# A hybrid DeltaNet and attention layer on one core: the first projection chunk in full fp32, the output projection by tokens, and the residual copied into the down projection's accumulators

## The chip, the cores and the metric

One core of a Trainium2 chip runs the whole layer. The metric is the time in microseconds from the first to the last moment of one execution on the device; three runs of the kernel before took 1507.93, 1508.70 and 1508.71 us (median 1508.7). The engines are TensorE (PE), VectorE (DVE), ScalarE (ACT) and GpSimd (POOL); SyncE (SP) issues most of the DMAs. Each engine works through a queue of its own in order, and engines wait for each other by semaphores.

## The reference

A decoder layer on 256 tokens (T) with 2048 channels (D), all in fp32. Two branches start from one projection of the normed input, are merged by sigmoid gates and go through an output projection; a gated MLP with a short convolution follows.

```python
h = rms_norm(x, ln1)
qkv_a, beta_a, decay_a, z_a, qkv_b, gate_a, gate_b = split_columns(h @ w_in)
y_a = gated_deltanet(qkv_a, beta_a, decay_a, z_a, ...) @ w_branch_a   # 8 heads of 128, causal conv of 4
y_b = moba_attention(q_b, k_b, v_b) @ w_branch_b                       # 8 heads of 128, partial rotary
x = x + (sigmoid(gate_a) * y_a + sigmoid(gate_b) * y_b) @ w_out
h = rms_norm(x, ln2)
u_gate, u_val = split(causal_dwconv(h @ w_up, ffn_conv, ffn_conv_bias))  # w_up is 2048 x 11264
x = x + (silu(u_gate) * u_val) @ w_down                                  # w_down is 5632 x 2048
return rms_norm(x, final_norm)
```

In the DeltaNet branch, a decay per head and token is `-exp(a_log) * softplus(a_logit + dt_bias)`, summed up along the tokens.

## The kernel before

**Matmuls.** The weights come from HBM as fp32 and each operand of a large matmul is split in two parts of type fp32r: a rounded high part and the rest. ScalarE makes the high part of a weight (`act.copy`, the CAST `wh<-wraw` of L118), VectorE the rest (`wl<-wraw,wh`, L115), and PE adds three products: high by high, high by rest, rest by high. `fetch` loads 1 MB of weights into one of four `wraw` buffers, `load_w` splits it in pieces. There are two ways to multiply:

- `chunk`: two blocks of 128 output channels. The weight is the stationary operand, the activations move, 256 tokens (or, where the PSUM pool is `wide`, high and rest side by side as 512 columns, so that two matmuls do the three products). The result has channels on the partitions.
- `by_token`: 512 output channels at a time. A tile of 128 tokens is stationary, the weights move 512 columns at a time. The result has tokens on the partitions.

**The norm.** The activations are only scaled by ln1 (`scaled`: high part on ScalarE L216, rest on VectorE L217, into `hc`). The factor of RMSNorm, R1, is applied to the results: by `join`, which copies and multiplies a chunk's PSUM result (tiles `un`, `unf`), or by a column `cols` of it per token. The sums of squares come from GpSimd (three pieces and one sum, L290 and L293) and ScalarE (one, L292); PE adds them over the partitions with two fp32 matmuls against `ones` (`R`), and a sqrt and a reciprocal follow.

**Stages in order.** (1) The input `xs` comes channel-major in eight pieces of 256 KB, alternating with eight pieces of the first two blocks of `w_gdn`; chunk q of DeltaNet group 0 is computed while they land (`ps_q0`). Then the small projection for beta and decay (`ps_bd`), R1, chunk k and chunk v; the decay chain on VectorE; a few small transposes (`pt_cols`) that turn decay, beta and R1 into columns. (2) For four groups of two heads: chunks q, k, v, and for every second group z by tokens (`ps_z`); then a generator `gdn` with the DeltaNet recurrence. (3) Four groups of MoBA attention (`ps_moba`, `ps_v`), also with generators. (4) Gates and branch projections by tokens (`ps_gate`, `ps_br`), merged and transposed (`pt_m`) to `mc`. (5) Output projection by chunks (`ps_wo`), residual added, squares, R2. (6) 44 up chunks (`ps_up`), convolution, silu, product into `acts`. (7) Down projection in eight PSUM banks `pd[i][n]`, 128 tokens by 512 channels each; the residual is transposed into them on PE by four 128x128 transposes a bank (L814). Then the last norm.

**What sets the order.** Instructions go out in program order unless a scheduler moves them by estimated times and priorities. Generators in the list `bg` (gdn, moba, rotary, merged) are advanced by `tick`, once for every 1700 ns of main matmuls (`main_mm`), so that their small instructions lie between the large matmuls. `while len(bg) > 1: tick()` after the third MoBA group runs all DeltaNet generators to their end, because the pool `gdn_st` is closed there and its space taken by the gates' tiles.

Of the kernel before, what the change touches and what calls it, by code (L numbers as in the profile page):

```python
# [11 lines left out]
F32 = mybir.dt.float32  # L12
# [7 lines left out]
P = 128  # L20
# [60 lines left out]
def layer_kernel(ctx: ExitStack, tc: tile.TileContext, xT, pos, cst, csel, ceye, vec, convw, ffw, bdv,  # L81
# [51 lines left out]
    def load_w(src, n=2048, into=None, piece=1024, raw=None):  # L133
        raw = raw or fetch(src, n)
        wh, wl = into or parts()
        for o in range(0, n, piece):
            split(wh[:, o:o + piece], wl[:, o:o + piece], raw[:, o:o + piece])
# [104 lines left out]
    wq = []  # L242
    for b in range(2):
        raw = wpool.tile([P, 2048], F32, name="wraw", tag="wraw", bufs=4)
        wq.append((raw, *parts()))
    for i in range(4):
        s = slice(4 * i, 4 * i + 4)
        for b in range(2):
            h = slice(4 * i + 2 * b, 4 * i + 2 * b + 2)
            sp.dma_start(xs[:, h, :], xT[:, h, :])  # L250
            sp.dma_start(wq[b][0][:, 512 * i:512 * i + 512], w_gdn[b][:, 512 * i:512 * i + 512])
    ps_q0 = mmt("ps_gdn")
    for i in range(4):
        scaled(xs[:, 4 * i:4 * i + 4, :], ln1v, 4 * i, hh, hl)
        for b in range(2):
            raw, wh, wl = (t[:, 512 * i:512 * i + 512] for t in wq[b])
            split(wh, wl, raw)
            for k in range(4):
                a = 4 * i + k
                main_mm(ps_q0[:, b], r3(wh, P)[:, k], hh[:, a], a == b == 0, False)  # L260
                main_mm(ps_q0[:, b], r3(wh, P)[:, k], hl[:, a], False, False)
                main_mm(ps_q0[:, b], r3(wl, P)[:, k], hh[:, a], False, a == KD - 1)
# [4 lines left out]
    raws = [fetch(w) for w in (w_gdn[2], w_gdn[3])]  # L267
# [15 lines left out]


    sq = []
    for i in range(4):
        sq.append(g.tile([P, 4, T], F32, name=f"sq1_{i}"))
        xv = xs[:, 4 * i:4 * i + 4, :]
        if i < 3:
            pool.tensor_tensor(sq[i], xv, xv, op=ALU.mult)  # L290
        else:
            act.activation(sq[i], xv, AF.Square)  # L292
    pool.tensor_tensor(sq[0], sq[0], sq[1], op=ALU.add)  # L293
# [639 lines left out]
```

## Time and profile before

| what | value |
|---|---|
| median of 3 runs | 1508.7 us (1507.93 to 1508.71) |
| the profiled execution, its time and its span | 1508.24 us, 1506.5 us |
| mean granted clock of TensorE | 0.996 |
| PE busy | 1482.6 us (98%) |
| DVE, ACT, POOL busy | 991.3 us (66%), 743.4 us (49%), 172.4 us (11%) |
| DMA traffic | 276.84 MB, mean 184 GB/s |

The span is the time between the first and the last instruction of the profiled execution; its own time is 1.7 us longer. Busy times are sums over the span, so a share of 66% can hold a stretch of 20 us in which the engine is never idle. Matmuls overlap each other in the records: the time that one costs is the distance between two starts, not its duration.

### The profile page before, as it was taken

The numbers are of one execution on the slowest core, as the hardware profiler recorded it, in microseconds if no ns is written. First come the engines' busy times: TensorE is split into PE (matmuls) and PEld (weight loads), VectorE is DVE, ScalarE is ACT, GpSimd is POOL, SyncE is SP. The second block draws the span as 40 slices with busy tenths as digits, with TensorE's granted clock in tenths as the row PEclk, the third lists the DMA queues.
The fourth block names the chain that finished last, engine by engine and source line by source line (L and its number), as shares of the span: only waits on it lengthen the run. The fifth ranks groups of instructions, "written<-read, shape, count | busy, mean of one in ns | idle before, by whom it ended". The sixth has DMA issues, their size and how long they took to land.

```text
span 1506.5 us, 21027 instructions
## 1 busy us (share of the span) xinstructions
PE 1482.6 (98%) x8507; PEld 1305.9 (87%) x8507; DVE 991.3 (66%) x1413; ACT 743.4 (49%) x997; POOL 172.4 (11%) x130
## 2 busy tenths in 40 slices
PE   7999999999999999999999999999999999999997
PEld 7899899998988888888888888888888888888886
DVE  8888668796655444666667677676776765555554
ACT  5565454435474444434455555554555554444444
POOL 3011001141203000000101212112111120000000
PEclk9999999999999999999999999999999999999999
DMA  8355444444445555546555555555555544555552
GB/s 312 141 198 190 163 154 157 149 169 147 154 154 174 193 194 194 193 177 249 186 208 196 184 188 188 196 196 182 188 189 196 196 177 162 195 195 194 195 196 84
DMA packets 43329, 276.84 MB, mean 184 GB/s; under 512 B 5248, under 2 KB 6736, under 8 KB 11104
## 3 DMA queue, kind: packets, MB, share of 16 engines
q1 hardware_dynamic: 41408, 270.98, 50.2%
q0 software_dynamic: 960, 2.36, 0.5%
q10 hardware_dynamic: 864, 2.16, 0.4%
q8 instruction: 66, 1.08, 0.3%
q14 instruction: 31, 0.25, 0.0%
HBM read 271.68 MB, written 3.80 MB: 183 GB/s over the span
## 4 chain that ended last, share of the span: by engine, by line
PE 92%; DVE 4%; ACT 1%; DMA 1%; issue 1%; SPq 0%; DVEq 0%; ACTq 0%; POOLq 0%
PE ps_up L108 32%; PE pd L96 16%; PE ps_gate L108 10%; PE ps_gdn L108 9%; PE ps_wo L108 6%; PE ps_br L108 6%; PE ps_moba L108 3%; PE ps_z L108 3%; PE ps_v L108 3%; DVE wl L115 2%; ACT wh L118 1%; DMA xs<-in_xT 1%; PE g L96 1%; PE pu L564 1%; PE py L558 1%
## 5 line engine op out<-in xcount | busy, mean ns | idle before, releaser
L115 DVE TENSOR_TENSOR wl<-wraw,wh 128x1024 fp32r<-128x1024 f32 (+1 forms) x504 | 603.3, 1233 | 275.4 <-ACT wh L118 274.8
L118 ACT CAST wh<-wraw 128x1024 fp32r<-128x1024 f32 (+1 forms) x504 | 500.1, 1039 | 411.3 <-PE ps_up L108 117.3
L108 PE MATMUL ps_up<-h,wh 128*128 128x512 f32 x1408 | 488.6, 390 | 0.0
L108 PE MATMUL ps_up<-h,wl 128*128 128x256 f32 x1408 | 397.0, 282 | 0.0
L108 PEld LDWEIGHTS ps_up<-h,wh 128*128 128x128 f32 x1408 | 264.2, 188 | 55.4
L108 PEld LDWEIGHTS ps_up<-h,wl 128*128 128x128 f32 x1408 | 266.1, 189 | 0.1
L108 PE MATMUL ps_gate<-wh,hc 128*128 128x512 f32 x512 | 156.0, 391 | 0.0
L108 PE MATMUL ps_gdn<-hc,wh 128*128 128x256 f32 x768 | 142.5, 287 | 8.8 <-ACT wh L118 6.0
L96 PE MATMUL pd<-wl,ah 128*128 128x512 f32 x336 | 130.8, 389 | 0.0
L96 PE MATMUL pd<-wh,al 128*128 128x512 f32 x336 | 130.8, 389 | 0.0
L108 PEld LDWEIGHTS ps_gdn<-hc,wh 128*128 128x128 f32 x768 | 121.7, 194 | 9.9 <-ACT wh L118 6.0
L800 POOL TENSOR_TENSOR acts<-sg,cvf 128x256 f32<-128x256 f32 x44 | 80.7, 1833 | 423.4 <-ACT sg L799 423.4
L108 PEld LDWEIGHTS ps_gate<-wh,hc 128*128 128x128 f32 x512 | 95.8, 188 | 19.7
L108 PE MATMUL ps_gdn<-hc,wl 128*128 128x256 f32 x384 | 110.2, 287 | 1.1 <-DVE wl L115 1.1
L794 ACT ACTIVATE cvf<-unf,ffv 128x256 f32<-128x256 f32 x88 | 48.2, 595 | 104.4 <-DVE unf L212 104.4
L796 DVE SCALAR_TENSOR_TENSOR cvf<-unf,ffv,cvf 128x254 f32<-128x254 f32 (+1 forms) x176 | 77.3, 480 | 32.1 <-ACT cvf L794 31.8
L108 PE MATMUL ps_gate<-wl,hc 128*128 128x512 f32 x256 | 97.1, 391 | 0.0
L108 PE MATMUL ps_moba<-hc,wh 128*128 128x256 f32 x512 | 93.1, 282 | 0.0
L96 PE MATMUL pd<-wh,ah 128*128 128x512 f32 x336 | 92.8, 391 | 0.0
L108 PE MATMUL ps_wo<-mc,wh 128*128 128x512 f32 x256 | 89.0, 390 | 0.4 <-ACT wh L118 0.4
L118 ACT CAST ah<-acts 128x256 fp32r<-128x256 f32 x44 | 17.9, 406 | 128.0 <-PE pd L96 118.3
L108 PEld LDWEIGHTS ps_moba<-hc,wh 128*128 128x128 f32 x512 | 78.7, 188 | 0.2
(420 smaller groups left out, 1881.5 us busy)
## 6 DMA issues: line engine op xcount, KB each, us to landing
wraw<-in_w_up SPq DMA_DIRECT2D x88, 1024.0 KB, 4.8
wraw<-in_w_dn SPq DMA_DIRECT2D x44, 1024.0 KB, 4.8
wraw<-in_w_gate SPq DMA_DIRECT2D x32, 1024.0 KB, 4.8
wraw<-in_w_gdn SPq DMA_DIRECT2D x22, 1024.0 KB, 4.9
wraw<-in_w_moba SPq DMA_DIRECT2D x16, 1024.0 KB, 5.0
wraw<-in_w_o SPq DMA_DIRECT2D x16, 1024.0 KB, 4.8
wraw<-in_w_z SPq DMA_DIRECT2D x8, 1024.0 KB, 4.8
wraw<-in_w_mv SPq DMA_DIRECT2D x8, 1024.0 KB, 4.8
```

The lines of the kernel that those rows point to most:

```text
L96: pe.matmul(ps, a, b, start=(start and i == 0), stop=(stop and i == n - 1), **kw)
L108: pe.matmul(ps, a, b, start=start, stop=stop, skip_group_check=True)
L115: (eng or dve).tensor_tensor(lo, src, hi.bitcast(F32), op=ALU.subtract)
L118: act.copy(hi, src)
L558: pe.matmul(py[:, p], ats[p], Tm[:, p], start=True, stop=True)
L564: pe.matmul(pu[:, p], Y[:, p, :], odd(U)[:, p], start=True, stop=True)
L794: act.activation(t[:, j, :], un[:, j, :], AF.Identity, scale=w[:, 2:3], bias=w[:, 3:4])
L796: dve.scalar_tensor_tensor(t[:, j, d:], un[:, j, :T - d], w[:, 2 - d:3 - d], t[:, j, d:], op0=ALU.mult, op1=ALU.add)
L800: pool.tensor_tensor(acts[:, c, :], sg, t[:, 1, :], op=ALU.mult)
```

## The change

1. **First chunk.** The weights come first in the alternating pieces, then xs. VectorE multiplies the raw weights by ln1 in place (8 pieces of 128x512, L263), and PE multiplies the raw weights and raw xs in fp32, 32 matmuls of 128x256 (L266) in place of 96 of type fp32r; no split of these weights. Ten fp32 matmuls `ones` by `ones` (`warm`, L249) stand ahead of all. Chunk k (`ps_k0`) follows at once, then ps_bd, R1 and chunk v. All four squares are on ScalarE, GpSimd has none.
2. **Decay.** The decay chain becomes a generator `decay` in `bg`, finished before DeltaNet group 0 begins; only R1's transposes stay ahead of ps_z. Group 0's generator is put into `bg` behind it.
3. **DeltaNet's end.** The pool is closed after the fourth MoBA group, not the third.
4. **Output projection** by tokens, four times 512 channels. x1 (the residual sum) is token-major, loaded by two DMAs of 1 MB; eight additions of 128x512 instead of sixteen of half a chunk each; 32 fp32 transposes on PE (`pt_x`, L774) feed `scaled` and the squares from PSUM, in four generators `normed`. The wide PSUM pool is set up after it. R2 is two fp32 matmuls of 512 columns, in the first up chunk.
5. **Down projection.** No transposes. Eight copies of x1 into the banks `pd`, four on ScalarE (L854) and four on VectorE (L856), in a changed order of banks.

```diff
+    warm = sdt("warm")
+    for i in range(10):
+        pe.matmul(warm[:, :P], ones, ones, start=True, stop=True)
...
+    for i in range(4):
+        for b in range(2):
+            h = slice(4 * i + 2 * b, 4 * i + 2 * b + 2)
+            sp.dma_start(wq[b][:, 512 * i:512 * i + 512], w_gdn[b][:, 512 * i:512 * i + 512])
+            sp.dma_start(xs[:, h, :], xT[:, h, :])
+    ps_q0 = mmt("ps_gdn")
     for i in range(4):
         s = slice(4 * i, 4 * i + 4)
         for b in range(2):
-            h = slice(4 * i + 2 * b, 4 * i + 2 * b + 2)
-            sp.dma_start(xs[:, h, :], xT[:, h, :])
-            sp.dma_start(wq[b][0][:, 512 * i:512 * i + 512], w_gdn[b][:, 512 * i:512 * i + 512])
-    ps_q0 = mmt("ps_gdn")
+            w = r3(wq[b], P)[:, s]
+            dve.tensor_tensor(w, w, ln1v[:, s, None].to_broadcast([P, 4, P]), op=ALU.mult)
+        for b in range(2):
+            for k in range(4 * i, 4 * i + 4):
+                pe.matmul(ps_q0[:, b], r3(wq[b], P)[:, k], xs[:, k], start=(k == b == 0), stop=(k == KD - 1),
+                          skip_group_check=True)
     for i in range(4):
         scaled(xs[:, 4 * i:4 * i + 4, :], ln1v, 4 * i, hh, hl)
-        for b in range(2):
-            raw, wh, wl = (t[:, 512 * i:512 * i + 512] for t in wq[b])
-            split(wh, wl, raw)
-            for k in range(4):
-                ...
+    ps_k0 = chunk([w_gdn[2], w_gdn[3]], hc, KD, "gdn", raws)
...
-            pool.tensor_tensor(sq[i], xv, xv, op=ALU.mult)
+        act.activation(sq[i], xs[:, 4 * i:4 * i + 4, :], AF.Square)
...
-        if gr == 2:
-            while len(bg) > 1:
-                tick()
-            gdn_st.close()
+    while gdns[-1] in bg:
+        tick()
+    gdn_st.close()
...
+    def normed(c):
+        yield
+        for n in (4 * c, 4 * c + 2):
+            pt = r3(sdt("pt_x"), T)
+            for j in range(2):
+                for i in range(2):
+                    pe.matmul(pt[:, j, i * P:(i + 1) * P], x1[:, i, (n + j) * P:(n + j + 1) * P], identb,
+                              start=(i == j == 0), stop=(i == j == 1), is_transpose=True, skip_group_check=True)
+            with tc.high_priority():
+                scaled(pt, ln2v, n, h2[:, :, 0, :], h2[:, :, 1, :])
+            ...
+    for c in range(4):
+        ps = by_token(w_o[4 * c:4 * c + 4], mc, KD, "ps_wo", flush=2 if c == 0 else None)
+        ...
+        for i in range(2):
+            xc = x1[:, i, c * 512:c * 512 + 512]
+            with tc.high_priority():
+                dve.tensor_tensor(xc, xc, ps[i], op=ALU.add)
+        bg.append(normed(c))
...
-    order = [(1, 2), (1, 3)] + [(0, n) for n in range(4)] + [(1, 0), (1, 1)]
-    def residual(i, n):
-        for j in range(4):
-            pe.matmul(pd[i][n][:, j * P:(j + 1) * P], x1[:, 4 * n + j, i * P:(i + 1) * P], identb,
-                      start=(j == 0), stop=False, is_transpose=True, skip_group_check=True)
+    order = [(1, 2), (1, 3), (1, 0), (1, 1), (0, 0), (0, 1), (0, 2), (0, 3)]
+    for e, (i, n) in enumerate(order):
+        o = x1[:, i, n * 512:n * 512 + 512]
+        if e % 2:
+            act.copy(pd[i][n], o)
+        else:
+            dve.tensor_copy(pd[i][n], o)
```

In the order of instructions, the brackets name the engine or the DMA queue that an instruction waits for. PE's queue at the start of the program, before:

```order
L108 MATMUL ps_gdn<-hc,wh 128x256 [waits Activation_49]
L108 MATMUL ps_gdn<-hc,wh 128x256 [waits DVE_49]
L108 MATMUL ps_gdn<-hc,wl 128x256 [waits DVE_49]
L108 MATMUL ps_gdn<-hc,wh 128x256 x2
L108 MATMUL ps_gdn<-hc,wl 128x256
L108 MATMUL ps_gdn<-hc,wh 128x256 [waits Activation_49]
```

and of the change, from the second row of the warm-up:

```order
L249 MATMUL warm<-ones 128x128 x9
L266 MATMUL ps_gdn<-xs,wraw 128x256 [waits DMAHW2_49,DMAHW1_49,DVE_49]
L266 MATMUL ps_gdn<-xs,wraw 128x256
L266 MATMUL ps_gdn<-xs,wraw 128x256 [waits DMAHW4_49]
L266 MATMUL ps_gdn<-xs,wraw 128x256
L266 MATMUL ps_gdn<-xs,wraw 128x256 [waits DMAHW3_49,DVE_49]
L266 MATMUL ps_gdn<-xs,wraw 128x256 x3
```

The third and fourth matmul of the first block wait for the fourth piece (DMAHW4, xs) and stand ahead of those of the second block, which need the third. Where R1 stands in PE's queue, before (`hc,wh` behind `ps_bd` is chunk k):

```order
L96 MATMUL ps_bd<-hc,wb_279 48x256 [waits DVE_49]
L96 MATMUL ps_bd<-hc,wb_279 48x256 x31
L108 MATMUL ps_gdn<-hc,wh 128x256 [waits Activation_49]
L108 MATMUL ps_gdn<-hc,wh 128x256
L108 MATMUL ps_gdn<-hc,wl 128x256 [waits DVE_49]
L96 MATMUL R_316<-sq_0_267,ones 128x256 [waits DVE_49]
L96 MATMUL R_316<-sq_0_267,ones 128x256
```

and of the change (`hc,wh` behind `R` is chunk v; the two rows ahead of `ps_bd` are the end of chunk k):

```order
L108 MATMUL ps_gdn<-hc,wh 128x256 x2
L108 MATMUL ps_gdn<-hc,wl 128x256
L96 MATMUL ps_bd<-hc,wb_323 48x256 [waits DVE_49]
L96 MATMUL ps_bd<-hc,wb_323 48x256 x31
L96 MATMUL R_360<-sq_0_311,ones 128x256 [waits DVE_49]
L96 MATMUL R_360<-sq_0_311,ones 128x256
L108 MATMUL ps_gdn<-hc,wh 128x256 [waits Activation_49]
```

R1 moved behind the whole of chunk k; only chunk v stands between it and ps_z now. PE's queue where the up projection ends (`pd1_2` is the bank of token half 1 and channels 1024 to 1535; `wh_11021`, `ah_11015` belong to the first of the 44 blocks), before:

```order
L108 MATMUL ps_up_10902<-h2_6056,wl_10946 128x256
L814 MATMUL pd1_2_11012<-identb_10997,x1_6157 128x128 [waits DMAHW3_49,DMAHW1_49]
L814 MATMUL pd1_2_11012<-identb_10997,x1_6157 128x128 x3
L96 MATMUL pd1_2_11012<-wh_11021,ah_11015 128x512 [waits Activation_49]
L96 MATMUL pd1_2_11012<-wl_11022,ah_11015 128x512 [waits DVE_49]
L96 MATMUL pd1_2_11012<-wh_11021,al_11016 128x512
L814 MATMUL pd1_3_11013<-identb_10997,x1_6157 128x128 [waits DMAHW2_49]
```

and of the change (`wh_10867` is of the first block, `wh_10903` of the second):

```order
L108 MATMUL ps_up_10742<-h2_5984,wl_10786 128x256
L96 MATMUL pd1_3_10851<-wh_10867,ah_10861 128x512 [waits Activation_49]
L96 MATMUL pd1_3_10851<-wl_10868,ah_10861 128x512 [waits DVE_49]
L96 MATMUL pd1_3_10851<-wh_10867,al_10862 128x512
L96 MATMUL pd1_3_10851<-wh_10903,ah_10897 128x512
L96 MATMUL pd1_3_10851<-wl_10904,ah_10897 128x512 [waits DVE_49]
L96 MATMUL pd1_3_10851<-wh_10903,al_10898 128x512
L96 MATMUL pd1_1_10849<-wh_10867,ah_10861 128x512 [waits PE_49,Activation_49]
```

The first down matmul waits for ScalarE now, and two blocks are done bank by bank. ScalarE's queue at that place, of the change; before, the same rows stood there without those of L854:

```order
L118 CAST wh_10903<-wraw_10901 128x1024 [waits DMAHW6_49,PE_49]
L118 CAST wh_10903<-wraw_10901 128x1024
L213 COPY unf_10823<-ps_up_10742 128x512 [waits PE_49]
L854 COPY pd1_3_10851<-x1_6134 128x512
L854 COPY pd1_1_10849<-x1_6134 128x512 [waits DVE_49]
L854 COPY pd0_1_10845<-x1_6134 128x512
L854 COPY pd0_3_10847<-x1_6134 128x512
L835 ACTIVATE cvf_10827<-unf_10823,ffv_6139 128x256 [waits DVE_49]
```

The copy into pd1_3 stands behind both casts of the second block and the copy of the last up chunk.

## Rows read from the trace of the kernel before

**Rows 1.** The page: busy time, share of the span and count of instructions of the engines (PE's line), and the chain of work that ended last, by engine.

```profile
PE 1482.6 (98%) x8507; PEld 1305.9 (87%) x8507; DVE 991.3 (66%) x1413; ACT 743.4 (49%) x997; POOL 172.4 (11%) x130
...
PE 92%; DVE 4%; ACT 1%; DMA 1%; issue 1%; SPq 0%; DVEq 0%; ACTq 0%; POOLq 0%
```

**Rows 2.** The waits of PE by what ended them: who waited, for whom, us in total, times, longest.

```profile
PE ps_gdn L108 <- ACT wh L118: 6.0, 1, 6.0
...
PE pd L814 <- DVE unf L210: 1.7, 1, 1.7
...
PE u L570 <- DVE U L565: 0.8, 1, 0.8
PE ps_z L108 <- DVE un L212: 0.7, 1, 0.7
PE ps_wo L108 <- DVE wl L115: 0.7, 1, 0.7
PE u L580 <- DVE vb L576: 0.7, 1, 0.7
...
PE ps_wo L108 <- ACT wh L118: 0.4, 1, 0.4
```

**Rows 3.** Windows of the start: busy us and instructions of each engine, then PEclk (the granted clock), DMA share and GB/s.

```profile
6.00:12.40 6.40, 5.72 (x24) 5.20 (x25) 5.64 (x8) 4.25 (x9) 3.16 (x2) 1.00 1.00 320
12.40:15.80 3.40, 1.85 (x12) 1.44 (x11) 3.40 (x2) 2.75 (x7) 3.32 (x2) 1.00 1.04 360
15.80:22.60 6.80, 5.12 (x22) 4.82 (x23) 6.80 (x11) 4.14 (x10) 2.30 (x2) 0.52 0.99 379
```

**Rows 4.** The timeline of PE in the first 34 us: start, duration, instruction, count, and in brackets the idle time before it and its releaser.

```profile
8.81 0.58 PE L108 MATMUL ps_gdn<-hc,wh 128*128 128x256 f32 x1 [0.68 <-DVE hc L217]
...
11.11 0.41 PE L108 MATMUL ps_gdn<-hc,wl 128*128 128x256 f32 x1
...
11.75 0.41 PE L108 MATMUL ps_gdn<-hc,wl 128*128 128x256 f32 x1
...
16.40 0.58 PE L108 MATMUL ps_gdn<-hc,wh 128*128 128x256 f32 x1 [1.88 <-DVE hc L217]
...
25.04 0.40 PE L108 MATMUL ps_gdn<-hc,wh 128*128 128x256 f32 x2
...
25.39 0.40 PE L108 MATMUL ps_gdn<-hc,wh 128*128 128x256 f32 x2
...
27.49 3.90 PE L96 MATMUL ps_bd<-hc,wb 128*48 128x256 f32 x32
...
31.59 1.03 PE L96 MATMUL R<-sq,ones 128*128 128x256 f32 x4
...
32.68 0.28 PE L108 MATMUL ps_gdn<-hc,wl 128*128 128x256 f32 x1
```

**Rows 5.** The timeline of ScalarE, VectorE, GpSimd (POOL) and SP in the first 20 us (SPq is the queue that issues DMAs; its row at 17.83 is the first that waits for the sixteenth piece).

```profile
8.81 0.62 ACT L118 CAST wh<-wraw 128x512 fp32r<-128x512 f32 x1 [1.44 <-DMA wraw<-in_w_gdn]
...
10.22 0.88 DVE L217 SCALAR_TENSOR_TENSOR hc<-xs,vc,hc 128x256 fp32r<-128x256 f32 x2
...
11.13 2.43 POOL L290 TENSOR_TENSOR sq<-xs 128x1024 f32<-128x1024 f32 x1 [2.67 <-DMA xs<-in_xT]
...
11.73 4.62 DVE L217 SCALAR_TENSOR_TENSOR hc<-xs,vc,hc 128x256 fp32r<-128x256 f32 x2
...
17.83 0.33 SPq L282 DMA_DIRECT2D eye<-in_ceye  x1
```

**Rows 6.** The timeline of VectorE and of PE behind the first chunks.

```profile
33.61 1.75 DVE L225 RECIPROCAL R<-R 128x256 f32<-128x256 f32 x1 [0.20 <-ACT R L224]
...
55.14 0.71 PE L108 MATMUL ps_z<-wh,hc 128*128 128x512 f32 x2
```

**Rows 7.** Windows of 20 us behind R, columns as in Rows 3.

```profile
40.00:60.00 20.00, 20.00 (x154) 19.01 (x153) 18.50 (x33) 8.66 (x11) 0.31 (x1) 1.00 0.48 166
60.00:80.00 20.00, 19.27 (x91) 15.50 (x90) 17.84 (x37) 14.40 (x17) 1.04 (x1) 1.00 0.38 139
```

**Rows 8.** Windows of 40 us inside the output projection and the gate stage, with the instructions of ps_wo and of ps_gate alone.

```profile
700.00:740.00 40.00, 40.00 (x233) 35.48 (x232) 4.13 (x6) 1.00 0.53 186
...
480.00:520.00 40.00, 40.00 (x178) 33.14 (x177) 2.74 (x4) 1.00 0.53 192
```

**Rows 9.** The timeline of all engines where the up projection ends and the down projection begins.

```profile
1252.79 0.28 PE L108 MATMUL ps_up<-h,wl 128*128 128x256 f32 x1
...
1252.99 2.00 ACT L118 CAST wh<-wraw 128x1024 fp32r<-128x1024 f32 x2 [0.58 <-PE ps_up L108]
...
1254.89 0.58 ACT L209 COPY unf<-ps_up 128x512 f32<-128x512 f32 x1
...
1256.35 0.68 DVE L210 TENSOR_TENSOR unf<-ps_up,unf 128x512 f32<-128x512 f32 x1
...
1257.09 0.66 PE L814 MATMUL pd<-identb,x 128*128 128x128 f32 x4 [1.74 <-DVE unf L210]
...
1258.28 0.60 PE L814 MATMUL pd<-identb,x 128*128 128x128 f32 x4
...
1259.42 0.60 PE L814 MATMUL pd<-identb,x 128*128 128x128 f32 x4
```

**Rows 10.** The window behind that turn, columns as in Rows 3.

```profile
1257.00:1270.00 13.00, 12.91 (x69) 10.84 (x70) 5.85 (x11) 4.83 (x9) 0.73 (x1) 1.00 0.32 104
```

More of the change, by code (lines that the diff above doesn't have):

```diff
@@ L136, in load_w @@
         for o in range(0, n, piece):
-            split(wh[:, o:o + piece], wl[:, o:o + piece], raw[:, o:o + piece])
+            lows.append(split(wh[:, o:o + piece], wl[:, o:o + piece], raw[:, o:o + piece]))
         return wh[:, :n], wl[:, :n]
@@ L615, in layer_kernel @@
         for a, t in enumerate((kq[:, 1], kq[:, 0], v)):
-            if gr == a == 0:
-                ps = ps_q0
+            if gr == 0 and a < 2:
+                ps = (ps_q0, ps_k0)[a]
             else:
-                ps = chunk(pair(w_gdn, 3 * gr + a), hc, KD, "gdn", *([raws] if (gr, a) == (0, 1) else []))
+                ps = chunk(pair(w_gdn, 3 * gr + a), hc, KD, "gdn")
             conv4(t, ps, 8 * a + h0)
+            if gr == 0 and a == 1:
+                bg.append(decay())
         if gr == 0:
-            cols = columns()
+            rms_columns()
         if gr % 2 == 0:
@@ L755, in layer_kernel @@
+    wide[0] = True
+    pst[2].close()
+    pst[2] = None
+    psum_pools(3, 2)
+    for c in range(NF):
         if c == 0:
             steps = ((0, 0, KD - 4), (1, 0, KD - 4), (0, KD - 4, KD), (1, KD - 4, KD))
-            ps = chunk(pair(w_o, c), mc, KD, "wo", steps=steps, flush=2)
-            y_st.close()
-            bkeep = bk.enter_context(tc.tile_pool(name="bkeep", bufs=1, side="right", reuse_waits="tile"))
-            x1 = bkeep.tile([P, KD, T], F32, name="x1")
-            ffv = bkeep.tile([P, 88, 4], F32, name="ffv")
@@ L779, in layer_kernel @@
[L779 to L788 removed]
+            ps = chunk([w_up[c], w_up[NF + c]], h2, KD, "up", steps=steps, flush=2)
@@ new lines, in layer_kernel @@
+            ps2 = sdt("R2")
+            mmg(ps2, [(ones, t) for t in sqs])
+            R2 = bkeep.tile([P, T], F32, name="R2")
+            act.copy(R2, ps2[:, :T])
+            dve.tensor_tensor(R2, R2, ps2[:, T:], op=ALU.add)
+            act.activation(R2, R2, AF.Sqrt, bias=epst, scale=1.0 / D)
+            dve.reciprocal(R2, R2)
+            R2b = both(R2)
+            bp.close()
+            m_st.close()
+            b = bk.enter_context(tc.tile_pool(name="b2", bufs=2, reuse_waits="tile"))
```

176 lines of the change are left out of this document (84 added, 92 removed).

## The prediction

> **What bounds the kernel now.** I read the page first. TensorE (PE) is busy 98% of the span and holds 92% of the chain that ended last, in matmuls of every stage [rows 1]. So time is won only where PE waits, runs at half clock, or has fewer or shorter matmuls to do. The waits by releaser say where it waits: 6.0 us before the first matmul, 1.7 where the down projection begins, and some of 0.4 to 0.8 us in the DeltaNet, z and output-projection stages [rows 2]. The windows of the start show the second loss: the granted clock reads 0.52 between 15.8 and 22.6 us [rows 3]. The timeline sharpens this. Three matmuls of 128x256 take 0.64 us at 11.11 and 0.35 us at 25.04 [rows 4]: 0.213 and 0.117 each, the levels of 1.2 and 2.4 GHz. By that pitch PE was at half clock from its first matmul too, until 12.4 us, although the clock column reads 1.00 there. It was full until 15.8, and fell again while PE sat idle for 1.88 us before 16.40 [rows 3, 4]. The first chunk's 96 matmuls need 11.2 us at full clock and end at 27.49.
>
> All predictions below are made on the profiled execution, 1508.24 us; the median of the runs is 1508.7, 0.46 higher, and I add that at the end. About 0.2% (3 us) is what a measurement of this kernel can tell from no change.
>
> **The start.** Between 31.59 and 32.68 lie the two fp32 matmuls of 128x256 (R) and two plain ones of 0.117 [rows 4]: 1.09 less 0.23 leaves 0.43 us each at full clock. The new chunk is 32 of these: 13.8 us on PE instead of 11.2, so PE work grows by 2.6. What goes is the wait for the split. VectorE needed 4.62 us for a pair of L217 (0.88 undisturbed) while GpSimd squared xs [rows 5]; the squares now stand on ScalarE and the fp32 matmuls wait for raw pieces and one VectorE multiply only. Pieces set the earliest times. The fourth was there at 8.81, when the cast that waited for it began, and the sixteenth at 17.83, when SP issued what waits for it [rows 5]. As I count it: warm-up from about 1 us (it needs only `ones`), two matmuls from about 5.3 (the first split, which needs more, let PE begin at 6.0 [rows 2]), a hole until piece four at 8.81, then 30 matmuls without a hole, because eight of them (3.4 us) outlast a group of four pieces (3.0 us: 9.02 from the fourth to the sixteenth). At full clock throughout they end at 21.7. The warm-up and the hole make me expect another stretch at half clock, at 0.86 us a matmul: with half clock until 12.4, as before, the end is 23.5; until 15, 24.8. I take 23.5. Then k chunk, ps_bd, R and v chunk follow as before, so the z stage begins at 51.1 instead of 55.14 [rows 6]: **-4.0** (-2.7 to -5.8).
>
> **VectorE behind R.** Before, R is computed in the second chunk, and 21.5 us lie between its reciprocal at 33.61 and the z stage [rows 6]. After, a whole chunk (k) comes ahead of R, so only some 10 us (one chunk less the sqrt) lie between. The un-joining and convolutions of q, k and v and the decay chain, all of which need R, move that much nearer to the weight splits of the z stage, which stand in the same VectorE queue. VectorE was busy 18.50 and 17.84 of 20 us there [rows 7], so 3.7 us of slack in 40, and PE already waited 0.7 for `un` [rows 2]. A pass of 40 us shortened by 4.0 leaves 0.3 too much. Nothing gained back from the pushed work is the one end (+0.3); the whole 4.0 lost again the other. The first DeltaNet matmuls, which stood in the z stage, move one stage later and give VectorE some room, so I take **+1.0**.
>
> **DeltaNet moved later.** The pool closes after the fourth MoBA group instead of the third. The two waits of the forced finish (0.8 `u<-U`, 0.7 `u<-vb`) can then be covered by the fourth group's matmuls: -1.5. The dependent steps may instead wait elsewhere; nothing in the trace prices it but such a wait again, 0.65 to 0.8 each. I take **-1.5**, with ends -1.5 and +3 (four more waits).
>
> **Output projection by tokens.** Before, 512 matmuls, at 40 us for 233 of them (0.1717): 87.9. After, 384 of 512 columns, at the pitch of ps_gate, 40/178 = 0.2247: 86.3 [rows 8]. That is -1.6. The 32 transposes come on top: in the down projection four of them with three matmuls take 1.14 us from 1258.28 to 1259.42, the three alone 0.67, so 0.117 each, +3.7 [rows 9]. Waits of 0.7 and 0.4 on `wl` and `wh` go [rows 2], since the last merged tiles are now needed only in the fourth block: -1.1. R2 needs as many columns as R did: nothing. At the turn to the up projection a transpose waits for VectorE's sum of the first token half; behind it stands all of the up projection, but nine matmuls (2.0 us) of the second half stand ahead and hide an add of about 0.7 (the unf add of rows 9 is such a one). If that cover fails the turn costs 0.7 per half. The x1 load waits for the last merge, as before, and its 2 MB are wanted only 22 us into the stage. Sum **+1.0** (-0.3 to +2.5).
>
> **Up to down.** Before: last up matmul 1252.79, then eight transposes and six matmuls, the wait to 1257.09, and six more groups of transposes at 0.47 [rows 9]. The overhead over the bare 24 matmuls is 8 x 0.47 + 1.74 = 5.5. After: PE's first down matmul waits for ScalarE's copy into pd1_3. ScalarE does two casts (2.00 from 1252.99) and the unf copy (0.58, ends 1255.47) ahead of it. A copy from SBUF into PSUM is not in the trace; the nearest row is that unf copy, the other way, 0.58, so I take 0.6 (ends: nothing, and twice that). PE resumes near 1256.1, 3.1 us after 1253.0. The second bank waits for VectorE's unf (1257.0) and a ScalarE copy to 1257.7, when six matmuls (1.35) are over at 1257.4: +0.3. Later copies, four on each engine at 0.6, are ahead of PE's 0.67 to 1.35 us a bank. Overhead 3.4, so -2.1.
>
> An idle PE of 3.1 us, however, is new. The clock fell with 1.88 us idle in the start [rows 4]; it did not with 1.74 at 1257 (the clock column reads 1.00 behind it [rows 10]). A longer hole than both lets me expect the fall. Its price: the half-clock stretch of the start was 6.8 us, which costs 3.4 in work not done; nothing is the other end. I take the middle, +1.7. So **-0.4** (-2.1 to +1.3). The Trainium skill, "TensorE: Matmul & The Clock Gate", Part 1, says the throttled state is the default and activity releases it, so a long idle PE falls back. By that rule the fall is to be expected; by the 1.74 us row alone the sum would be 1.7 lower. Rows at 15.8 to 22.6 agree with the rule.
>
> **Sum.** -4.0 + 1.0 - 1.5 + 1.0 - 0.4 = -3.9. 1508.24 - 3.9 = 1504.3 profiled, 1504.8 as a median.
>
> **The rivals.**
> *No clock loss* (0.20): the warm-up holds the full clock through the first chunk (-1.8) and the 3.1 us hole does not drop it (-1.7): 1501.3. For it: the fp32 chunk leaves PE no hole after 8.81. Against: the hole before 8.81.
> *VectorE becomes the bound behind R* (0.17): the start's 4.0 are given back by late `wl` and late `cols`: 1504.8 + 3.0 = 1507.8. For it: 18.50 of 20 busy.
> *The start does not gain* (0.06): pieces come later when weights go first, and the chunk ends at 27.5 as now: 1508.8.
> *Slower, by the clock* (0.07): the holes while pieces land keep PE at half clock through all 32 fp32 matmuls. Thirty at 0.86 from 8.81 end at 34.6, 11.1 later than I expect: 1515.9. Without the start's -4.0 the sum is +0.1, so the sign turns to slower by 3 us once the chunk ends after 27.49 + 2.9 = 30.4, that is if the clock does not rise before about 26. Against: before, the clock rose at 12.4, when PE had worked from 8.81 on without a hole [rows 3, 4].
> *Slower, by DeltaNet* (0.05): drained after the last group with little behind it, its chain costs PE some nine waits of 0.7: 1504.8 + 1.5 + 6.3 = 1512.6.
>
> **How the numbers follow.** My forecast gets 0.45, with a range of its own from 1502.5 to 1507 (three quarters of it under 1505.7, the bound for faster). Faster: 0.34 + 0.20 = 0.54. Same: 0.11 + 0.17 + 0.06 = 0.34. Slower: 0.12. The range leaves out the two slower cases and a little of the fast one's far side: 1499.5 to 1509.5.
>
> **What would show it.** Right: ps_q0's last fp32 matmul near 23.5, z stage near 51; the granted clock with one more half stretch at the start and one near the first pd matmul; PE's first pd matmul about 3.1 us after the last ps_up, released by ScalarE; transposes in the output projection at 0.12 us with no wait over 0.7 us around them; ps_wo stage about 1 us longer. Wrong: PE waits of over 1 us on VectorE between 50 and 80 us; a chunk end past 27; waits on DeltaNet tiles near the close of its pool. The likeliest error is in the clock, which decides 3.5 us.

## The result and the profile after

The changed kernel takes 1499.94 us (median of 4 runs, 1499.04 to 1500.39) against 1508.32 us of the kernel before beside it (1507.70 to 1508.71): a ratio of 0.9942, 95% interval 0.9930 to 0.9954. That is 8.4 us faster. Forecast was 1504.8, range 1499.5 to 1509.5, so the time is inside at the fast end, and the gain is about twice the 3.9 us that the steps had summed to. The profiled execution of the change took 1500.10 us, its span is 1498.3.

The page of the change, busy time by engine and the chain by engine (before: [rows 1]):

```profile
PE 1484.5 (99%) x8363; PEld 1301.6 (87%) x8363; DVE 979.8 (65%) x1412; ACT 741.0 (49%) x995; POOL 161.2 (11%) x126
...
PE 96%; DVE 2%; DMA 1%; ACT 0%; issue 0%; DVEq 0%; SPq 0%; ACTq 0%
```

PE is busy for 1.9 us more in a span 8.2 us shorter; VectorE's share of the chain fell from 4% to 2%, ScalarE's from 1% to nothing. All waits of PE that the profile lists (before: [rows 2]):

```profile
PE pd L96 <- ACT pd L854: 2.9, 1, 2.9
PE warm L249 <- POOL ones L147: 1.0, 1, 1.0
PE ps_gdn L266 <- DMA xs<-in_xT: 0.6, 1, 0.6
PE ps_v L108 <- DVE wl L115: 0.6, 1, 0.6
PE ps_gate L108 <- DVE qk L216: 0.3, 1, 0.3
```

The waits of the first chunk on ScalarE and VectorE, those on `un` and `u`, and both of the output projection are gone ([rows 2]), and so are two on `pT` that the profile of the kernel before lists:

```profile
PE pT L662 <- DVE s__3694 L656: 0.5, 1, 0.5
PE pT L662 <- DVE s__4149 L656: 0.4, 1, 0.4
```

The small ones on `ps_v` and `ps_gate` are new, and one is larger: 2.9 us where the down projection begins, 1.7 before.

The starts of PE's stages, read from the timelines of the two kernels, show where the 8.2 us of span were won:

| first instruction of | before | after | difference |
|---|---|---|---|
| z stage | 55.14 | 49.82 | -5.3 |
| branch projections | 581.92 | 574.01 | -7.9 |
| output projection | 672.85 | 663.87 | -9.0 |
| up projection | 763.73 | 754.87 | -8.9 |
| last up matmul | 1252.79 | 1245.36 | -7.4 |
| last down matmul | 1498.04 | 1489.79 | -8.25 |

So -5.3 in the start, -2.6 from the z stage to the end of the gates, +0.5 from there through the up projection, -0.8 at the turn to the down projection.

### The profile page after: what moved, and what is told of

It is laid out like the page before. It is cut to its first block, busy times and chain, and to the rows that moved or that the text cites. A ratio compares the mean times of both kernels' runs of the same rounds, so it can differ in the third digit from the quotient of the medians.

```text
span 1498.3 us, 20734 instructions
## 1 busy us (share of the span) xinstructions
PE 1484.5 (99%) x8363; PEld 1301.6 (87%) x8363; DVE 979.8 (65%) x1412; ACT 741.0 (49%) x995; POOL 161.2 (11%) x126
## 4 chain that ended last, share of the span: by engine, by line
PE 96%; DVE 2%; DMA 1%; ACT 0%; issue 0%; DVEq 0%; SPq 0%; ACTq 0%
PE ps_up L108 33%; PE pd L96 16%; PE ps_gate L108 12%; PE ps_gdn L108 8%; PE ps_wo L108 6%; PE ps_br L108 6%; PE ps_moba L108 5%; PE ps_z L108 3%; PE ps_v L108 3%; DMA wraw<-in_w_gdn 1%; DVE wl L115 1%; PE py L567 1%; PE g L96 1%; PE pu L573 1%; PE t L559 0%; DVE tm L537 0%
## 5 line engine op out<-in xcount | busy, mean ns | idle before, releaser
L115 DVE TENSOR_TENSOR wl<-wraw,wh 128x1024 fp32r<-128x1024 f32 x496 | 600.1, 1246 | 286.1 <-ACT wh L118 285.5
L118 ACT CAST wh<-wraw 128x1024 fp32r<-128x1024 f32 x496 | 495.2, 1046 | 384.6 <-PE ps_up L108 117.6
L108 PE MATMUL ps_gdn<-hc,wh 128*128 128x256 f32 x704 | 126.1, 281 | 0.0
L96 PE MATMUL pd<-wh,al 128*128 128x512 f32 x336 | 125.4, 391 | 0.0
L96 PE MATMUL pd<-wl,ah 128*128 128x512 f32 x336 | 125.3, 391 | 0.0
L108 PEld LDWEIGHTS ps_gdn<-hc,wh 128*128 128x128 f32 x704 | 107.9, 188 | 0.7
L108 PE MATMUL ps_gdn<-hc,wl 128*128 128x256 f32 x352 | 98.9, 281 | 0.1
L108 PE MATMUL ps_wo<-wh,mc 128*128 128x512 f32 x256 | 79.5, 393 | 0.0
```

Of the source, the lines that this page charges most:

```text
L96: pe.matmul(ps, a, b, start=(start and i == 0), stop=(stop and i == n - 1), **kw)
L108: pe.matmul(ps, a, b, start=start, stop=stop, skip_group_check=True)
L115: return (eng or dve).tensor_tensor(lo, src, hi.bitcast(F32), op=ALU.subtract)
```

## The experiments

Times are medians; "the change" is at 1499.9, the kernel before between 1508.3 and 1508.6 in all comparisons. The 95% interval of a ratio reaches 0.0009 to 0.0014 to each side, which is 1.4 to 2 us; smaller differences are read from the profiles or left open.

### The parts one by one

**Start alone.** Part 1 (warm-up, fp32 chunk, squares on ScalarE, chunk k ahead of R1) put into the kernel before; the decay chain stays in place:

```diff
+            dve.tensor_tensor(w, w, ln1v[:, s, None].to_broadcast([P, 4, P]), op=ALU.mult)
...
+                pe.matmul(ps_q0[:, b], r3(wq[b], P)[:, k], xs[:, k], start=(k == b == 0), stop=(k == KD - 1),
+                          skip_group_check=True)
...
+    ps_k0 = chunk([w_gdn[2], w_gdn[3]], hc, KD, "gdn", raws)
...
-            pool.tensor_tensor(sq[i], xv, xv, op=ALU.mult)
+        act.activation(sq[i], xs[:, 4 * i:4 * i + 4, :], AF.Square)
```

> The kernel before with part 1 of the change alone (warm-up, fp32 first chunk, squares on ScalarE, chunk k ahead of R1). The decay chain stays where it was, ahead of the transposes pt_cols, and so ahead of the z stage. Theory A (the start's 5.3 us come through only because the decay chain was moved out of the way): R1 comes one chunk later, the chain behind it takes VectorE about 19 us (35.4 to 54.2 in the kernel before), and only one chunk of 11.2 us is left to cover it. PE then waits some 7 to 9 us ahead of pt_cols, and the time is 0 to 4 us above that of the kernel before. Rival B (the start's gain is independent of the decay chain): the z stage begins 4 to 5.5 us earlier and the whole is 4 to 6 us faster.

Measured: 1509.9 us, ratio 1.0009 (1.0001 to 1.0018). PE's timeline ahead of the z stage, the window around it (columns as in Rows 3), and the only waits of PE that its timeline shows from 60 us to the end of the gates:

```profile
56.49 0.28 PE L423 MATMUL pt_cols<-ct,gc 16*128 16x16 f32 x1 [6.32 <-DVE gc L345]
...
52.80:63.00 10.20, 6.36 (x20) 5.08 (x21) 8.22 (x20) 3.66 (x7) 0.67 (x2) 0.50 0.35 130
...
156.06 0.63 PE L556 MATMUL t<-ct,U 128*128 128x128 f32 x4 [0.40 <-DMA U<-dU]
...
355.06 0.50 PE L108 MATMUL ps_v<-wl,hc 128*128 128x512 f32 x1 [0.56 <-DVE wl L115]
...
404.96 0.73 PE L108 MATMUL ps_gate<-wh,hc 128*128 128x512 f32 x2 [0.26 <-DVE qk L216]
```

The z stage began at 57.67, 2.5 us later than before: PE stood 6.3 us for the decay chain (`gc`), a little less than the 7 to 9 expected, and the clock was at half behind that. Twelve matmuls of the z stage took 5.26 us from 57.67 and 2.75 us from 63.67 on, so the stretch cost another 2.5 us. Theory A holds.

The waits on `u` and `pT` are gone here too, although the decay chain stands where it was. From the z stage to the branch projections this kernel needs 527.1 us, 524.6 without the half-clock stretch; the kernel before needs 526.8 and the change 524.2.

**Start and decay.** Parts 1 and 2 together; to the edit above comes

```diff
+    def decay():
...
+            if gr == 0 and a == 1:
+                bg.append(decay())
+        while gr == 0 and bg:
+            tick()
```

> The kernel before with parts 1 and 2: the start, and the decay chain as a background generator finished behind the z stage. Theory A: z stage begins 5.3 us earlier as in the full change, the wait of 0.9 us for un in the z stage is gone, and the time is 5.5 to 7 us below that of the kernel before. The prediction on record, with VectorE giving back 1.0: 3 us. If VectorE gives back more (its rival), there are PE waits of over 1 us between 50 and 85 us, and the gain stays under 2 us.

Measured: 1499.3 us, ratio 0.9944 (0.9931 to 0.9956): the whole gain, and 2 us more than the 7 us at the far end of my theory. The z stage began at 49.54, as in the change. Two of the five executions, the profiled one (1501.6) among them, were 1.5 and 2.3 us above the median.

**Decay alone.** Part 2 without the rest, the second edit without the first:

```diff
+            if gr == 0 and a == 1:
+                bg.append(decay())
         if gr == 0:
-            cols = columns()
+            rms_columns()
...
+        while gr == 0 and bg:
+            tick()
```

> The kernel before with part 2 alone: the decay chain as a background generator, finished behind the z stage, so that the DeltaNet generators begin one stage later. Theory: the waits of PE on the DeltaNet tiles in the kernel before (0.9 for un in the z stage, 1.0 and 0.8 near 323 and 331 us, 0.6 twice in the gates) go because all of the recurrence lies later against the large matmuls, not because the pool is closed later: 2 to 3 us faster than the kernel before. Rival: they are tied to the start, and alone this part gives at most the 0.9 in the z stage.

Measured: 1505.4 us, ratio 0.9978 (0.9970 to 0.9987), 3.2 us faster. PE's waits, from the fifth on:

```profile
PE ps_wo L108 <- DVE wl L115: 0.7, 1, 0.7
PE ps_v L108 <- DVE wl L115: 0.6, 1, 0.6
PE ps_wo L108 <- ACT wh L118: 0.4, 1, 0.4
PE ps_gate L108 <- DVE qk L216: 0.3, 1, 0.3
```

The waits on `un`, `u` and `pT` are not there; 0.6 on `ps_v` and 0.3 on `ps_gate` are new. The z stage began at 54.95, the branch projections 2.85 us earlier than before. So part 2 alone takes the DeltaNet waits away; but so does part 1 alone, as shown above, so neither is their one cause. What the two have in common can be read from the profiles: the first matmul of `u` starts 134.5 us after the first of the z stage in the three profiles that have these waits (the kernel before and the next two runs below), and 140.6 us after it with part 2, in the change too (143.6 with part 1 alone, of which its half-clock stretch is 2.5). That the recurrence, some 6 us later against the large matmuls, finds cover there is the likely way; no run moved it by itself.

**The later closing alone.** Part 3 without the rest:

```diff
-        if gr == 2:
-            while len(bg) > 1:
-                tick()
+    while gdns[-1] in bg:
+        tick()
```

> The kernel before with part 3 alone: the DeltaNet generators are run to their end after the fourth MoBA group instead of the third. Theory A: the two PE waits of 0.99 and 0.81 us near 323 and 331 us go, the rest of the DeltaNet work is covered by the fourth group: 1.5 to 2 us faster. Rival: the waits only move, to a forced finish behind the fourth group: within 0.5 us of the kernel before.

Measured: 1508.4 us, ratio 1.0000 (0.9991 to 1.0009). The waits stayed where they were:

```profile
PE u L580 <- DVE vb L576: 0.7, 1, 0.7
PE u L570 <- DVE U L565: 0.6, 1, 0.6
```

The rival was right in the time, not in the reason: the waits did not move, and from the z stage to the branch projections the kernel needs 526.7 us, before 526.8.

**Output and down projection alone.** Parts 4 and 5 without the rest:

```diff
+        ps = by_token(w_o[4 * c:4 * c + 4], mc, KD, "ps_wo", flush=2 if c == 0 else None)
...
-                if k == 0:
-                    residual(i, n)
+            act.copy(pd[i][n], o)
...
+            dve.tensor_copy(pd[i][n], o)
```

> The kernel before with parts 4 and 5 alone: output projection by tokens, residual copied into the accumulators. From the two traces I expect: 1.0 won ahead of and in the output projection (the waits of 0.65 and 0.82 us go, transposes and shorter matmuls nearly cancel), 1.4 lost at the first up chunk (R2 and the last transposes), 0.8 won at the turn to the down projection, where PE idles 3 us and then runs a stretch at half clock. Sum: 0.4 us faster, within 1 us of the kernel before. The prediction on record: 1.0 - 0.4, 0.6 us slower. A rival that gives these parts the larger share of the 8.4 us: more than 2 us faster.

Measured: 1508.7 us, ratio 1.0002 (0.9993 to 1.0011). No measurable share. Its executions lie far apart, 1506.1 to 1510.9; the profiled one is the fastest of them and has the highest mean granted clock (0.999, the others 0.993 to 0.997). It has the same 2.9 us wait at the turn and a clock column of 1.00 behind it. From the last up matmul to the last down matmul it needs 243.2 us, the kernel before 245.25 and the change 244.4.

### What in the start

**Split or fp32, GpSimd or ScalarE.** Three kernels complete a table of two by two. Split first chunk in the change:

```diff
-            dve.tensor_tensor(w, w, ln1v[:, s, None].to_broadcast([P, 4, P]), op=ALU.mult)
...
+            split(wh, wl, raw)
+            for k in range(4):
+                a = 4 * i + k
+                main_mm(ps_q0[:, b], r3(wh, P)[:, k], hh[:, a], a == b == 0, False)
+                main_mm(ps_q0[:, b], r3(wh, P)[:, k], hl[:, a], False, False)
+                main_mm(ps_q0[:, b], r3(wl, P)[:, k], hh[:, a], False, a == KD - 1)
```

> The changed kernel with the first chunk in three fp32r products as before (weights split by ScalarE and VectorE), everything else as in the change: warm-up, order of pieces, squares on ScalarE, decay behind. It tells the fp32 matmuls apart from the removal of GpSimd's squares. Theory (fp32 matters): ScalarE has 16 scalings of 0.46, 8 casts of 0.6 and 4 squares of 1.04, 16 us from 6.2 on, so the chunk ends near 24.5 instead of 22.0, and the kernel is 2 to 3 us slower than the change. Rival (the slow VectorE pairs beside GpSimd were all there was to win): chunk end within 0.7 us of the change, time too.

The same with GpSimd's squares:

```diff
-        act.activation(sq[i], xs[:, 4 * i:4 * i + 4, :], AF.Square)
+        if i < 3:
+            pool.tensor_tensor(sq[i], xv, xv, op=ALU.mult)
+        else:
+            act.activation(sq[i], xv, AF.Square)
+    pool.tensor_tensor(sq[0], sq[0], sq[1], op=ALU.add)
```

> The changed kernel with the first chunk split as before and three of the four squares and a sum back on GpSimd. Against the run with the split chunk and squares on ScalarE (z stage at 50.3 us) it shows what GpSimd's squares cost the split. Theory (they are the cause of the start's loss): VectorE pairs of up to 4.6 us beside GpSimd are back, the chunk ends 3 to 5 us later, z stage near 54, and the kernel takes 1503.5 to 1505.5. Rival: they cost the chunk nothing, z stage at 50 to 51, 1500 to 1501; then the order of pieces or of the chunks is what the start gained by.

And GpSimd's squares beside the fp32 chunk:

> The changed kernel, fp32 first chunk as it is, with three of the four squares and a sum back on GpSimd. Theory: the multiply of the weights and the scalings on VectorE have two inputs from SBUF and are slowed beside GpSimd as the split is, but the fp32 matmuls wait for one multiply only and not for the scalings, so the chunk ends 1 to 2 us later than in the change, and the second chunk, which needs the scalings, at most 2 to 3: 1501 to 1503. Rival: fp32 makes the chunk independent of VectorE, z stage within 0.5 us of the change.

Measured, with the start of the z stage in the profile:

| first chunk | squares on ScalarE | three squares on GpSimd |
|---|---|---|
| fp32 | 1499.94 us, z at 49.8 (the change) | 1505.68 us, z at 55.4 |
| split | 1500.66 us, z at 50.3 | 1507.70 us, z at 57.4 |

From one row of the table to the other it is 0.7 to 2.0 us, from one column to the other 5.7 to 7.0. With the squares on ScalarE the rival was right on fp32: it hardly matters. GpSimd, which here has a sum of two squares besides, costs more than I expected in both. VectorE in the split chunk, squares on ScalarE:

```profile
10.70 0.88 DVE L221 SCALAR_TENSOR_TENSOR hc<-xs,vc,hc 128x256 fp32r<-128x256 f32 x2
11.53 0.69 DVE L115 TENSOR_TENSOR wl<-wraw,wh 128x512 fp32r<-128x512 f32 x1
```

and with three squares on GpSimd:

```profile
11.54 2.50 DVE L221 SCALAR_TENSOR_TENSOR hc<-xs,vc,hc 128x256 fp32r<-128x256 f32 x2
13.97 2.86 DVE L115 TENSOR_TENSOR wl<-wraw,wh 128x512 fp32r<-128x512 f32 x1
...
11.62 2.15 POOL L301 TENSOR_TENSOR sq<-xs 128x1024 f32<-128x1024 f32 x1 [1.94 <-DMA xs<-in_xT]
13.85 2.44 POOL L304 TENSOR_TENSOR sq<-sq,sq 128x1024 f32<-128x1024 f32 x1
```

A pair of scalings takes 2.50 instead of 0.88 and a `wl` piece 2.86 instead of 0.69, while a GpSimd instruction of 2.2 to 2.4 us runs. The fp32 chunk did not escape it: one of its multiplies takes 2.83 us and others wait in VectorE's queue behind such pairs, and PE waits for them, here with the window behind the longest wait:

```profile
PE ps_gdn L266 <- DVE wraw L263: 3.7, 2, 3.2
...
16.30:22.00 5.70, 5.69 (x13) 4.55 (x14) 5.70 (x10) 3.85 (x5) 1.70 (x1) 0.50 1.01 404
```

The clock is part of the price: behind that wait of 3.2 us it was at half for 5.7 us, in which PE did 13 matmul records; in the change it did 29 in the same window. My estimate from this row is 2.9 us, half of the 5.7.

With the split and GpSimd's squares the z stage begins 2.3 us later than in the kernel before, which has both (55.14). So with these two the new order of pieces and chunks wins nothing; no run moved the squares alone in the kernel before.

**No warm-up:**

```diff
-    for i in range(10):
-        pe.matmul(warm[:, :P], ones, ones, start=True, stop=True)
```

> The changed kernel without its ten warm-up matmuls. In the profile of the change PE runs from 1.0 us and the clock is full from 10.0 us, so eight of the 64 records of the fp32 chunk are at half clock. Theory: without the warm-up PE starts at 6.3 and the clock rises later, 12 to 14 us as in the kernel before; each us at half clock costs 0.5 us of the chunk, so 1 to 2 us slower than the change (1501 to 1502). Rival: the warm-up does nothing, since PE is at half clock until about 10 us either way: within 0.5 us of the change.

Measured: 1499.6 us, ratio 0.9942 (0.9929 to 0.9954). The rival: it does nothing that shows. By the pitch of the matmuls the clock was full from 11.2 us without it and from 10.0 with it, and chunk k began at 22.35 and 21.83; the z stage began at 49.86 and 49.82.

This profile tells more about the turn to the down projection. It has the same wait of 2.94 us there as the change, and its first down matmul starts at 1248.59 (the change: 1248.58), but the clock stayed full behind it:

```profile
1249.10:1252.50 3.40, 3.36 (x15) 2.42 (x15) 3.37 (x6) 2.67 (x5) 0.00 (x0) 1.00 0.72 224
```

In the change the same window has 9 matmuls at 0.50. The last down matmul starts at 1488.55 here and at 1489.79 in the change, so the fall of the clock costs 1.24 us.

### The turn from up to down

**Filled hole, first try.** Thirteen small fp32 matmuls (ones by ones) in front of the copies, into bank (1,2). The columns of that bank come out wrong, so this kernel does not compute the layer and stands here for its time alone.

```diff
+    for i in range(13):
+        pe.matmul(pd[1][2][:, :P], ones, ones, start=True, stop=True)
```

> The changed kernel with thirteen fp32 matmuls of 128x128 (ones by ones, 2.8 us at full clock) put into PE's hole at the turn from up to down projection, into a bank whose copy comes late. The hole stays as long as it is; only PE is not idle in it. Theory: the half-clock stretch of 3.4 us behind the hole goes, and the kernel is 1.7 us faster than the change in those executions that had it: median 1498 to 1498.5, and a narrower spread. Rival: the clock behind the hole makes no difference to the end, because copies set the pace of the banks there: within 0.4 us of the change.

Measured: 1501.2 us, 1.2 slower than the change. It is no test of the clock: the order of the banks changed, and PE waited for the copy into bank (1,2) instead.

```profile
1245.08 3.06 PE L852 MATMUL pd<-ones 128*128 128x128 f32 x26
...
1250.69 0.47 PE L96 MATMUL pd<-wh,ah 128*128 128x512 f32 x1 [1.53 <-DVE pd L858]
...
1251.40:1254.70 3.30, 3.30 (x9) 2.53 (x9) 2.50 (x7) 1.32 (x4) 0.74 (x1) 0.50 0.38 161
```

After 26 records of fp32 matmuls in 3.06 us, three large matmuls and 1.53 us of waiting the clock fell all the same, to 0.50.

**Filled hole, second try.** Twelve matmuls of the large kind, 128x512, into the bank that is filled last:

```diff
+    for i in range(12):
+        pe.matmul(pd[0][0], h2[:, 0, 0, :P], h2[:, 0], start=True, stop=True, skip_group_check=True)
```

> The changed kernel with twelve matmuls of 128x512 of the large kind (2.7 us) in PE's hole at the turn from up to down projection, into the bank that is filled last, (0,0), with the order of the first copies as in the change. Theory: the hole is as long as before, the clock stays full behind it, and the kernel is 1.3 to 1.7 us faster than the change, about 1498.4. Rival: no difference to the end within 0.5 us, or the clock falls all the same.

Measured: 1498.6 us (1498.2 to 1499.4), 1.3 faster than the change (1499.0 to 1500.4), so the two overlap. PE's timeline and the window behind:

```profile
1244.62 2.89 PE L852 MATMUL pd<-h 128*128 128x512 f32 x12
1247.72 0.50 PE L96 MATMUL pd<-wh,ah 128*128 128x512 f32 x1 [0.21 <-ACT pd L856]
...
1249.00:1256.00 7.00, 6.94 (x30) 5.12 (x29) 5.49 (x12) 4.95 (x10) 0.73 (x1) 1.00 0.42 152
```

The down projection begins as long after the last up matmul as in the change (3.2 us from 1244.50), the clock column reads 1.00, and the medians differ by the 1.3 us at the lower bound of the theory. In the profiles it is less: from the last up matmul to the last down matmul 243.4 us, against 244.4 in the change.

**Two banks filled early.** The best version. Two banks are taken from the small PSUM pool once R2 is through, and filled during the third up chunk:

```diff
+            sd_st.close()
+            ps_e = ctx.enter_context(tc.tile_pool(name="ps_e", bufs=1, space=PSUM, side="right", reuse_waits="tile"))
+            pd_e = [ps_e.tile([P, 512], F32, name=f"pd1_{n}") for n in (2, 3)]
...
+            if c == 2:
+                act.copy(pd_e[1], x1[:, 1, 1536:2048])
+                dve.tensor_copy(pd_e[0], x1[:, 1, 1024:1536])
```

> The changed kernel, but two of the eight accumulator banks (token half 1, channels 1024 to 2047) are taken over from the small PSUM pool after R2 and filled with the residual during the up projection. PE can then begin the down projection in these banks at once. Theory: the hole of 2.9 us at the turn breaks up into waits of about 0.7, 1.0 and 0.3 us (casts and rest of the second block, then the next copy), 1.4 us less in all, and the clock no longer falls there, another 1.7 us: 3 us faster than the change, about 1497. Rival: the clock falls all the same, 1.4 us faster. Second rival: the waits just move behind the second block's split, and nothing is won.

Measured: 1497.35 us (1497.1 to 1497.9), ratio 0.9928 (0.9914 to 0.9941): 2.6 us under the change, all executions under its fastest, and 11.3 under the kernel before. PE at the turn:

```profile
1244.84 0.28 PE L108 MATMUL ps_up<-h,wl 128*128 128x256 f32 x1
1244.96 0.63 PE L96 MATMUL pd<-wh,ah 128*128 128x512 f32 x2
...
1247.09 0.73 PE L96 MATMUL pd<-wh,ah 128*128 128x512 f32 x2 [0.59 <-ACT wh L118]
1248.54 0.50 PE L96 MATMUL pd<-wl,ah 128*128 128x512 f32 x1 [0.72 <-DVE wl L115]
...
1245.00:1256.00 11.00, 9.66 (x41) 7.05 (x40) 7.44 (x12) 5.97 (x10) 0.74 (x1) 1.00 0.49 183
```

The down projection begins without a wait; 0.59 and 0.72 us remain on the casts and `wl` of the second block, and the clock stays at 1.00. From the last up matmul to the last down matmul it needs 242.1 us, 2.4 less than the change.

## Why the prediction was right, and its size was not

The direction came out, and the time lies 0.4 us inside the fast end of the range. That it lies inside is in part luck: this end was opened for a rival in which the clock stays full in the first chunk and behind the turn, and neither happened. The gain beyond the forecast has other sources.

**Start: -4.0 forecast, -5.3 measured.** Right in sign and place, mis-sized by the pieces and the clock. PE ran like this, first the warm-up, then the fp32 chunk (before: [rows 4]):

```profile
1.00 4.64 PE L249 MATMUL warm<-ones 128*128 128x128 f32 x20 [1.00 <-POOL ones L147]
6.27 15.91 PE L266 MATMUL ps_gdn<-xs,wraw 128*128 128x256 f32 x64 [0.63 <-DMA xs<-in_xT]
21.83 0.58 PE L108 MATMUL ps_gdn<-hc,wh 128*128 128x256 f32 x2
```

I had put the fourth piece at 8.81, as it was before, and a hole ahead of it. It was there when PE needed it; the 64 records lie in one run from 6.27. The clock was full from 10.0, not 12.4, with no second fall. The chunk was over at 21.8 instead of 23.5. That this is the time that I gave for a full clock throughout (21.7) is chance: no hole, but half clock until 10.0.

The reason that I named was only partly the right one. I wrote that the wait for the split goes. The table of two by two shows that in the new order this wait is made by GpSimd, and a fall of the clock behind it: with the squares on ScalarE the z stage begins almost as early behind a split chunk (50.3). The row was there, 4.62 against 0.88 [rows 5]; I took it as one disturbance, where in the new order it is worth more than the fp32 chunk. The Trainium skill, "SBUF — State Buffer", section "SBUF: two separate sides", says that VectorE and GpSimd share a port pair by an exclusive lock, so that of a VectorE instruction with two SBUF inputs and a GpSimd instruction that reads SBUF the later one blocks until the other is through. The rows 2.50 and 2.86 beside 2.15 and 2.44 agree with it.

**VectorE behind R: +1.0 forecast, nothing measured.** The decay's place was the condition. The start alone lost 1.4 us, with PE 6.3 us behind the chain that I had called pushed; with the chain behind the z stage the profile lists no wait of PE for VectorE between 22 and 340 us. VectorE was no busier (before: [rows 7]):

```profile
40.00:60.00 20.00, 20.00 (x130) 18.09 (x130) 18.03 (x30) 14.20 (x18) 1.04 (x1) 1.00 0.30 110
60.00:80.00 20.00, 20.00 (x122) 17.66 (x121) 17.48 (x32) 11.21 (x15) 0.00 (x0) 1.00 0.64 231
```

What left the z stage, the first DeltaNet work, is the room that I had named, and gave too little; that it was enough is read from these rows, no run tested it alone.

**DeltaNet: -1.5 forecast; with the wait on `un` -2.6 measured, by another cause.** I tied it to the later closing of the pool. That alone gave nothing, so this step failed in its mechanism, and that a gain came here all the same is luck. Part 2, which I costed under VectorE only, gave 3.2 us alone, and part 1 alone has nearly as much as the change in these stages (524.6 us against 526.8 before, without its half-clock stretch; the change 524.2). Both shift the recurrence against the large matmuls; why part 1 does so stays open.

**Output projection: +1.0 forecast, +0.5 measured** to the second up chunk. The wait of 0.4 ahead of it went, and four transposes (`pt_m`) moved from there into the stage (together -1.1 at its first matmul, in the table of stages). The stage itself came out even (+0.1), shorter matmuls and the second wait against the transposes. R2 and the last transposes stand in the first up chunk now, where the stages differ by +1.4; I had costed R2 at nothing because its columns are the same, and it only changed place.

**Up to down: -0.4 forecast, -0.8 measured,** the step that came out best. PE's first down matmul, what ScalarE did before it, and the window behind (before: [rows 9, 10]):

```profile
1245.36 0.28 PE L108 MATMUL ps_up<-h,wl 128*128 128x256 f32 x1
1245.56 1.99 ACT L118 CAST wh<-wraw 128x1024 fp32r<-128x1024 f32 x2 [0.58 <-PE ps_up L108]
...
1247.46 0.58 ACT L213 COPY unf<-ps_up 128x512 f32<-128x512 f32 x1
1247.94 0.59 ACT L854 COPY pd<-x 128x512 f32<-128x512 f32 x1
...
1248.58 0.50 PE L96 MATMUL pd<-wh,ah 128*128 128x512 f32 x1 [2.94 <-ACT pd L854]
...
1249.10:1252.50 3.40, 3.40 (x9) 2.64 (x9) 3.37 (x6) 2.65 (x5) 0.00 (x0) 0.50 0.66 231
```

Casts, the unf copy and the copy into the bank take the order and durations that I gave them, 3.1 us forecast and 3.2 measured, and the clock fell for 3.4 us. The two terms of the step can be told apart. Where the clock stayed full, in the profile of the output and down projection alone, the turn is 2.1 us shorter than before (243.2 against 245.25), as I had it. I priced the fall at 1.7; the profile without the warm-up says 1.24, which makes the -0.8. Whether the clock falls differs from one profile to the next. The rule of the Trainium skill, "TensorE: Matmul & The Clock Gate", Part 1, that a long idle PE falls back, held in this profile; it did not in those two, with the same wait. The copy from SBUF into PSUM, which no row of before had, takes 0.59.

By the runs, then, parts 1 and 2 are the whole: 9.1 us by the medians. Parts 3 to 5 give nothing that can be measured; the forecast had them at -0.9 together. The 4.3 us missing in my sum lie in the first three steps: 1.3 in the start, 1.0 behind R, 1.1 with `un` in the DeltaNet stages; the rest, 0.9, in the last two.

## What to carry to other kernels

A slow pair of instructions on one engine beside a busy other one is worth an experiment of its own: in the changed kernel, three squares on an engine that was half busy instead of one that was otherwise idle are worth 5.7 to 7.0 us, the new arithmetic beside it 0.7 to 2.0. A part that only makes room (here the decay chain, moved behind a stage) can decide whether another part gains or loses, so parts are to be tried together and apart. Where an accumulator waits for a copy at a turn between stages, look for banks that are free long before.

## What the runs showed of the hardware

- The clock behind a wait differs from one profile to the next, though the code there and the wait are the same. With 2.94 us of wait at the turn, it fell in the profiles of the change and of the three kernels of the table; it did not in that without the warm-up, nor in that of the output and down projection alone, whose executions lie 4.8 us apart.
- It also fell without a wait. In the kernel with start and decay, PE ran eight matmul records of 64 columns, then eight of a single column (`ssq`), then four of 16 rows (`bc_g`), from 212.8 to 215.2, and the window behind reads half. The change runs the same records from 213.0 to 215.5, and the clock stays full. So neither these matmuls nor the wait alone decides it, and what does is open.

```profile
212.75 1.00 PE L567 MATMUL py<-Tm,aq 128*128 128x64 f32 x8
213.59 1.00 PE L469 MATMUL ssq<-ones,sqq 128*128 128x1 f32 x8
...
215.60:219.00 3.40, 3.40 (x19) 3.40 (x18) 3.40 (x12) 2.62 (x3) 0.00 (x0) 0.50 0.11 46
```

  The change in the same window:

```profile
215.60:219.00 3.40, 3.40 (x30) 3.40 (x31) 3.40 (x13) 2.78 (x4) 0.31 (x1) 1.00 0.20 82
```

- In the start the clock column reads 1.00 before PE has reached its full pitch. In the change 18 matmul records of the fp32 chunk fall between 6.3 and 12 us and 30 between 12 and 18, under the same 1.00; the kernel before does the same until 12.4 us:

```profile
6.00:12.00 6.00, 5.73 (x18) 4.76 (x19) 3.91 (x8) 3.88 (x8) 0.00 (x0) 1.00 0.98 320
12.00:18.00 6.00, 6.00 (x30) 5.28 (x29) 6.00 (x13) 5.33 (x11) 0.00 (x0) 1.00 1.05 397
```
